# The first SwiGLU chunk of an encoder layer takes its weight sums from the last stage's two buffers

## The chip, the cores and the metric

The kernel runs on one core of one Trainium2 chip. The metric is device time in microseconds (us), the median of the runs shown.

## What is computed

One post-norm encoder layer over 256 positions of width 2048, in float32: a combined projection feeding a convolution group, a pooling group and a Fourier group, an output projection, LayerNorm, then the part that matters here:

```
hid = silu(x @ w_gate) * (x @ w_up)            # 2048 -> 5632
ffn = hid @ w_down                             # 5632 -> 2048
ple = sigmoid(x @ w_ple_gate) * (p @ w_ple)
x   = layer_norm(ALPHA * x + ffn + ple, ln2_g, ln2_b)
```

## The kernel before

Weights stream from HBM as tiles of 128 x 2048 float32 (1 MB). Every tile is taken apart into a high and a low part: a cast on ACT (`whi`, L125) and a subtraction on DVE (`wlo`, L126), each on half a tile (128 x 1024). For every 128 rows of weights `mm3` (L163 to L165) then issues three 128x128x512 matmuls on PE: high by high, low by high, high by low.

All streamed weight tiles go through the pool `wraw`, which has four buffers with the name `raw`. SP issues the loads in one queue; a load waits until the buffer's last reader is done, and the loads behind it wait with it.

The stage ahead of SwiGLU is the gate projection of `ple` (`w_pg`, four chunks of 512 columns). Each of its chunks ends with a sigmoid on ACT (L543), a product with `ple` (L544) and an update of the residual (L545) on DVE. Its tiles (`sg2`, `ple0`, `ple1` and others) are in the pool `ple`. When this pool and the pool `conv` are closed, the last stage's pool `ffn` is laid over the same memory.

SwiGLU (`hidden`) goes over 11 chunks of 512 hidden columns. Each chunk makes the two products x W_gate and x W_up as a Strassen-like scheme, for which sums of weight tiles are needed: `b11` is gate tile 0, `b12` is up tile 0, and `tsum = b11 + b12` is made by DVE (L592). After that a DMA from POOL adds up tile 1 onto `b12` in place (L593). Later `tsum` gets `b22` (up tile 1) added (L604) and then, by another POOL DMA, gate tile 1 (L606). So `b12` and `tsum` are held for most of a chunk. In chunks 1 to 10 they are in `ffn`, in two buffers named `sraw`. In chunk 0 they are two of the four `raw` buffers, and the other tiles of chunk 0 pass through the two that are left.

PE's order in a chunk is: `b11` (12 matmuls onto X), `tsum` (12, onto Z), up tile 2 (24), `tsum` again (12), `b22` (12), up tile 3 (24), `b12` (12), then gate tile 2 (24), gate tile 1 (12), `tsum` (12) and gate tile 3 (24): 180 in all. The order of instructions on each engine is fixed when the program is built.

Of the kernel before, what the change touches and what calls it, by code (L numbers as in the profile page):

```python
# [9 lines left out]
F32 = mybir.dt.float32  # L10
# [6 lines left out]
P = 128  # L17
# [7 lines left out]
NC = 512  # L25
# [63 lines left out]
def encoder_layer(ctx: ExitStack, tc, t):  # L89
    nc = tc.nc  # L90
    cpool = ctx.enter_context(tc.tile_pool(name="const", bufs=1))
    wraw = ctx.enter_context(tc.tile_pool(name="wraw", bufs=4))
# [27 lines left out]
    def load(out, in_):  # L120
        last_load[0] = nc.sync.dma_start(out, in_)
# [427 lines left out]
    with tc.tile_pool(name="ffn", bufs=1) as ffn:  # L549
        st = [small.tile([P, 8, 6], F32, name=f"st2{j}", tag=f"st2{j}") for j in range(NT)]  # L550

        def x1q(j, q):

            a = slice((q % 2) * 4, (q % 2) * 4 + 4)
            return x1hi[q // 2][:, a, j * P : (j + 1) * P], x1lo[q // 2][:, a, j * P : (j + 1) * P]

        def form(i):
            return fhi[:, i], flo[:, i]

        def fetch(dram, u, pool, tag, bufs):  # L560
            raw = pool.tile([P, 4 * NC], F32, name=tag, tag=tag, bufs=bufs)
            load(raw, dram[u])
            return raw

        def multiply(raw, uses):

            for h in range(0, 4, 2):
                hi = wsp.tile([P, 2, NC], F32R, name="whi", tag="whi")
                lo = wsp.tile([P, 2, NC], F32R, name="wlo", tag="wlo")
                split(raw[:, h * NC : (h + 2) * NC].rearrange("p (k n) -> p k n", n=NC), hi, lo)  # L570
                for k in range(2):
                    for out, (ahi, alo), start, stop in uses:
                        mm3(
                            out, ahi[:, h + k, :], alo[:, h + k, :], hi[:, k, :], lo[:, k, :],
                            start and h + k == 0, stop and h + k == 3, skip_group_check=True,
                        )

        def kept(src):
            out = ffn.tile([P, NC], F32, name="sgl", tag="sgl", bufs=6)
            nc.scalar.copy(out, src)  # L580
            return out

        def hidden(c, pool, tag, bufs):


            acc = lambda: pacc.tile([P, NC], F32, name="acc", tag="acc")
            gate, up = t["w_gate"][c], t["w_up"][c]
            X, Z = acc(), acc()
            b11 = fetch(gate, 0, wraw, "raw", None)
            b12 = fetch(up, 0, pool, tag, bufs)  # L590
            tsum = pool.tile([P, 4 * NC], F32, name=tag, tag=tag, bufs=bufs)
            nc.vector.tensor_tensor(tsum, b11, b12, op=ALU.add)  # L592
            nc.gpsimd.dma_start(b12, up[1], accum_op=ALU.add)  # L593
            multiply(b11, [(X, x1q(0, 0), True, True)])
            W = acc()
            nc.scalar.copy(W, X)
            multiply(tsum, [(Z, form(0), True, True)])
            while deferred:
                deferred.pop(0)()
            s5 = kept(Z)  # L600
            V = acc()
            multiply(fetch(up, 2, wraw, "raw", None), [(V, x1q(1, 2), True, False), (Z, x1q(0, 2), False, False)])
            b22 = fetch(up, 1, wraw, "raw", None)
            nc.vector.tensor_tensor(tsum, tsum, b22, op=ALU.add)  # L604
            multiply(tsum, [(X, form(1), False, True)])
            nc.gpsimd.dma_start(tsum, gate[1], accum_op=ALU.add)  # L606
            s16 = kept(X)
            multiply(b22, [(Z, form(3), False, False)])
            multiply(fetch(up, 3, wraw, "raw", None), [(V, x1q(1, 3), False, True), (Z, x1q(0, 3), False, True)])
            multiply(b12, [(X, form(2), False, True)])  # L610

            nc.vector.tensor_tensor(s16, Z, s16, op=ALU.subtract)
            nc.vector.tensor_tensor(s5, s5, X, op=ALU.subtract)
            nc.vector.tensor_tensor(s5, V, s5, op=ALU.add)
            multiply(fetch(gate, 2, wraw, "raw", None), [(W, x1q(0, 2), False, False), (X, x1q(1, 2), False, False)])
            multiply(fetch(gate, 1, wraw, "raw", None), [(W, x1q(0, 1), False, False)])
            multiply(tsum, [(X, x1q(1, 1), False, False)])
            multiply(fetch(gate, 3, wraw, "raw", None), [(W, x1q(0, 3), False, True), (X, x1q(1, 3), False, True)])
            hh = ffn.tile([P, 4, S], F32R, name="hhi", tag="hhi", bufs=4)
            hl = ffn.tile([P, 4, S], F32R, name="hlo", tag="hlo", bufs=4)  # L620

            def end():
                sg = gates(c)
                for s, p in zip(sg, (W, X)):
                    nc.scalar.activation(s, p, AF.Silu)
                gated(c, sg, (s16, s5), hh, hl)

            deferred.append(end)
            return hh, hl

        def gates(c):

            tag, bufs = ("keep", 2) if c in PAIRS else ("sgl", 6)
            return [ffn.tile([P, NC], F32, name=tag, tag=tag, bufs=bufs) for _ in range(NT)]
# [7 lines left out]
        def gated(c, g, v, hh, hl):  # L642

            for j in range(NT):
                nc.vector.tensor_tensor(g[j], v[j], g[j], op=ALU.mult)
                if c not in PAIRS or j == 0:
                    js = slice(j * P, (j + 1) * P)
                    turn(g[j], hh[:, :, js], hl[:, :, js])
            if c in PAIRS:
                first[:] = [g, hh, hl]  # L650
            if c - 1 in PAIRS:
                (a11, a21), ph, pl = first
                a12, a22 = g
                fh, fl = (ffn.tile([P, 3, 4, P], F32R, name=n, tag=n) for n in ("dfh", "dfl"))
                tail = slice(P, S)
                for a, b, op, out, hi, lo in (
                    (a21, a22, ALU.subtract, a22, ph[:, :, tail], pl[:, :, tail]),
                    (a11, a21, ALU.subtract, a21, fh[:, 1], fl[:, 1]),
                    (a22, a11, ALU.subtract, a11, fh[:, 0], fl[:, 0]),
                    (a12, a11, ALU.add, a12, fh[:, 2], fl[:, 2]),  # L660
                ):
                    nc.vector.tensor_tensor(out, a, b, op=op)
                    turn(out, hi, lo)
                sums_of[c - 1] = [(ph[:, :, tail], pl[:, :, tail])] + [(fh[:, i], fl[:, i]) for i in range(3)]
# [50 lines left out]

        first, sums_of = [], {}
        for part in ((0, 4), (4, 8), (8, 11)):
            hid = [hidden(c, *((ffn, "sraw", 2) if c else (wraw, "raw", None))) for c in range(*part)]
            if part[1] == 11:
                g2, b2 = (ffn.tile([P, D], F32, name="sraw", tag="sraw", bufs=2) for _ in range(2))  # L720
                for b, row in ((g2, t["ln2_g"]), (b2, t["ln2_b"])):
                    nc.sync.dma_start(b, row.partition_broadcast(P))
            nk = 4 * len(hid)
            last = part[1] == 11
            if not last:
                for c in (0, 2):
                    down_pair(c, part[0], hid)
                continue
            for c in range(4):
                ps = project(  # L730
                    t["w_down"][c][part[0] : part[1]], nk,
                    lambda k: (hid[k // 4][0][:, k % 4, :], hid[k // 4][1][:, k % 4, :]),
                    behind=16 if c == 3 else 0, spare=12 if c == 3 else 0, halves=c == 3,
                )
                for j in range(NT):
                    for h in range(2):
                        cc = slice(c * NC + h * S, c * NC + (h + 1) * S)
                        src = ps[j][:, h * S : (h + 1) * S] if j == 0 or c < 3 else ps[1 + h][:, :S]
                        nc.vector.tensor_tensor(res[j][:, cc], src, res[j][:, cc], op=ALU.add)
                        nc.vector.bn_stats(st[j][:, 2 * c + h, :], res[j][:, cc])  # L740
# [108 lines left out]
```

## Time and profile before

| what | value |
|---|---|
| median of 3 runs | 1079.39 us (1079.01 to 1079.45) |
| the profiled execution: its time | 1079.06 us |
| the profiled execution: its span | 1077.3 us |
| PE busy | 1055.2 us (98%) |
| DVE busy | 878.7 us (82%) |
| ACT busy | 646.5 us (60%) |
| mean rate of the DMAs | 229 GB/s |

The span is the time between the first and the last instruction of the profiled execution; 1.8 us of its time lie outside the span. PE is a chain of matmuls with short gaps, so what counts is where PE waits, and for whom.

### The profile page before, as it was taken

The numbers are of one execution on the slowest core, as the hardware profiler recorded it, in microseconds if no ns is written. First come the engines' busy times: TensorE is split into PE (matmuls) and PEld (weight loads), VectorE is DVE, ScalarE is ACT, GpSimd is POOL, SyncE is SP. The second block draws the span as 40 slices with busy tenths as digits, with TensorE's granted clock in tenths as the row PEclk, the third lists the DMA queues.
The fourth block names the chain that finished last, engine by engine and source line by source line (L and its number), as shares of the span: only waits on it lengthen the run. The fifth ranks groups of instructions, "written<-read, shape, count | busy, mean of one in ns | idle before, by whom it ended". The sixth has DMA issues, their size and how long they took to land.

```text
span 1077.3 us, 12568 instructions
## 1 busy us (share of the span) xinstructions
PE 1055.2 (98%) x4692; PEld 857.5 (80%) x4692; DVE 878.7 (82%) x1021; ACT 646.5 (60%) x810; POOL 30.9 (3%) x56
## 2 busy tenths in 40 slices
PE   7999999999999999999999999999999999999995
PEld 6888878887788878888887888888887878888884
DVE  5899999969956768888879778798788787887576
ACT  6888876636644656666655556566655565665440
POOL 0000000000000000000000000000000000000000
PEclk9999999999999999999999999999999999999998
DMA  9777543644554788678787786777787877868432
GB/s 355 283 280 219 196 156 137 241 159 177 196 195 159 227 274 302 210 239 270 233 273 224 246 294 199 252 262 231 245 248 259 273 212 249 291 199 321 176 115 78
DMA packets 36801, 246.62 MB, mean 229 GB/s; under 512 B 4188, under 2 KB 4740, under 8 KB 7940
## 3 DMA queue, kind: packets, MB, share of 16 engines
q1 hardware_dynamic: 32004, 212.25, 51.5%
q0 software_dynamic: 4736, 33.57, 16.8%
q8 instruction: 37, 0.61, 0.2%
q14 instruction: 24, 0.20, 0.1%
HBM read 243.70 MB, written 2.10 MB: 228 GB/s over the span
## 4 chain that ended last, share of the span: by engine, by line
PE 90%; DVE 6%; DMA 1%; ACT 1%; issue 1%; SPq 0%; DVEq 0%; ACTq 0%
PE acc L164 29%; PE acc L163 29%; PE acc L165 29%; DVE wlo L126 2%; PE tp L639 1%; ACT whi L125 1%; DMA raw<-in_w_gate 1%; DMA raw<-in_w_in 1%; PE tp L448 1%; DVE res L744 0%; DVE res L749 0%; DVE sraw L695 0%; DVE sraw L604 0%; DVE res L506 0%; PE tp L403 0%
## 5 line engine op out<-in xcount | busy, mean ns | idle before, releaser
L126 DVE TENSOR_TENSOR wlo<-raw,whi 128x1024 fp32r<-128x1024 f32 (+1 forms) x354 | 423.5, 1214 | 116.4 <-ACT whi L125 112.7
L125 ACT CAST whi<-raw 128x1024 fp32r<-128x1024 f32 (+1 forms) x354 | 369.7, 1048 | 234.8 <-PE acc L165 212.2
L163 PE MATMUL acc<-whi,ahi 128*128 128x512 f32 x1108 | 435.3, 395 | 6.8 <-ACT whi L125 5.5
L164 PE MATMUL acc<-wlo,ahi 128*128 128x512 f32 x1108 | 435.0, 393 | 1.0 <-DVE wlo L126 0.9
L165 PE MATMUL acc<-whi,alo 128*128 128x512 f32 x1108 | 431.6, 391 | 0.1
L163 PEld LDWEIGHTS acc<-whi,ahi 128*128 128x128 f32 x1108 | 208.6, 188 | 54.9 <-ACT whi L125 6.4
L164 PEld LDWEIGHTS acc<-wlo,ahi 128*128 128x128 f32 x1108 | 208.5, 188 | 48.4 <-DVE wlo L126 6.6
L165 PEld LDWEIGHTS acc<-whi,alo 128*128 128x128 f32 x1108 | 208.4, 188 | 43.6 <-DVE alo L126 0.4
L125 ACT CAST whi<-sraw 128x1024 fp32r<-128x1024 f32 x112 | 116.5, 1053 | 91.6 <-PE acc L165 55.3
L126 DVE TENSOR_TENSOR wlo<-sraw,whi 128x1024 fp32r<-128x1024 f32 x112 | 135.0, 1221 | 43.5 <-ACT whi L125 43.1
L164 PE MATMUL acc<-wlo,hhi 128*128 128x512 f32 x264 | 104.5, 396 | 0.0
L165 PE MATMUL acc<-whi,hlo 128*128 128x512 f32 x264 | 103.6, 395 | 0.0
L163 PE MATMUL acc<-whi,hhi 128*128 128x512 f32 x264 | 103.5, 397 | 0.0
L281 ACT ACTIVATE pr<-uT,par 128x256 f32<-128x256 f32 x128 | 56.8, 501 | 5.6 <-DVE part L283 5.4
L163 PEld LDWEIGHTS acc<-whi,hhi 128*128 128x128 f32 x264 | 49.6, 188 | 12.7 <-DVE res L676 1.2
L164 PEld LDWEIGHTS acc<-wlo,hhi 128*128 128x128 f32 x264 | 49.7, 188 | 12.1 <-DVE wlo L126 1.0
L165 PEld LDWEIGHTS acc<-whi,hlo 128*128 128x128 f32 x264 | 49.7, 188 | 11.6
L287 DVE SCALAR_TENSOR_TENSOR mixc<-uT,par,mixc 128x256 f32<-128x256 f32 x104 | 46.4, 474 | 0.0
L283 DVE TENSOR_TENSOR part<-part,pr 128x512 f32<-128x512 f32 x64 | 43.5, 680 | 0.3 <-ACT pr L281 0.2
L592 DVE TENSOR_TENSOR sraw<-raw,sraw 128x2048 f32<-128x2048 f32 x10 | 22.9, 2292 | 0.3
L604 DVE TENSOR_TENSOR sraw<-sraw,raw 128x2048 f32<-128x2048 f32 x10 | 22.9, 2286 | 0.1
L580 ACT COPY sgl<-acc 128x512 f32<-128x512 f32 x22 | 12.9, 588 | 14.5 <-PE acc L165 13.2
(148 smaller groups left out, 630.2 us busy)
## 6 DMA issues: line engine op xcount, KB each, us to landing
raw<-in_w_gate SPq DMA_DIRECT2D x44, 1024.0 KB, 7.3
raw<-in_w_down SPq DMA_DIRECT2D x40, 1024.0 KB, 5.0
raw<-in_w_up SPq DMA_DIRECT2D x34, 1024.0 KB, 4.9
raw<-in_w_in SPq DMA_DIRECT2D x22, 1024.0 KB, 5.0
raw<-in_w_out SPq DMA_DIRECT2D x16, 1024.0 KB, 4.8
raw<-in_w_pg SPq DMA_DIRECT2D x16, 1024.0 KB, 4.9
sraw<-in_w_up SPq DMA_DIRECT2D x10, 1024.0 KB, 6.9
sraw<-in_w_up POOLq DMA_DIRECT2D x10, 1024.0 KB, 9.3
```

The lines of the kernel that those rows point to most:

```text
L125: nc.scalar.copy(hi, src)
L126: return nc.vector.tensor_tensor(lo, src, hi.bitcast(F32), op=ALU.subtract)
L163: nc.tensor.matmul(out, ahi, whi, start=start, stop=False, **more)
L164: nc.tensor.matmul(out, ahi, wlo, start=False, stop=False, **more)
L165: nc.tensor.matmul(out, alo, whi, start=False, stop=stop, **more)
L281: nc.scalar.mul(pr[:, n, :], uT[ch][:, k : k + S], w)
L283: nc.vector.tensor_tensor(part, part, pr, op=ALU.add)
L287: nc.vector.scalar_tensor_tensor(y[ch], in0=uT[ch][:, k : k + S], scalar=w, in1=y[ch], op0=ALU.mult, op1=ALU.add)
L448: nc.tensor.matmul(out, ones, x, start=i == 0, stop=i == NCH - 1)
L580: nc.scalar.copy(out, src)
L592: nc.vector.tensor_tensor(tsum, b11, b12, op=ALU.add)
L604: nc.vector.tensor_tensor(tsum, tsum, b22, op=ALU.add)
```

## The change

Chunk 0 takes `b12` and `tsum` from `ffn` like the other chunks. The parameters that told the chunks apart are gone.

```
-        def hidden(c, pool, tag, bufs):
+        def hidden(c):
...
             b11 = fetch(gate, 0, wraw, "raw", None)
-            b12 = fetch(up, 0, pool, tag, bufs)
-            tsum = pool.tile([P, 4 * NC], F32, name=tag, tag=tag, bufs=bufs)
+            b12 = fetch(up, 0, ffn, "sraw", 2)
+            tsum = ffn.tile([P, 4 * NC], F32, name="sraw", tag="sraw", bufs=2)
             nc.vector.tensor_tensor(tsum, b11, b12, op=ALU.add)
             nc.gpsimd.dma_start(b12, up[1], accum_op=ALU.add)
...
-            hid = [hidden(c, *((ffn, "sraw", 2) if c else (wraw, "raw", None))) for c in range(*part)]
+            hid = [hidden(c) for c in range(*part)]
```

The buffers of a pool are laid out in the order in which they are first asked for. `sraw` was first asked for in chunk 1, behind `sgl`, `hhi` and `hlo`; now it is the first of `ffn`.

SP's queue, from the load of `b11` (raw_3085) on. Before, with `b12` as raw_3087 and the first `sraw` load that of chunk 1 (sraw_3390); what a load waits for is in brackets (DVE and Activation are counts of those engines' instructions, DMAHW and DMASW those of earlier DMAs):

```order
L121 DMA raw_3085<-in_w_gate 128x2048 [waits DMAHW5_49,DVE_49]
L121 DMA raw_3087<-in_w_up 128x2048 [waits DMAHW6_49,DVE_49]
L121 DMA raw_3137<-in_w_up 128x2048 [waits DMAHW0_49,DVE_49]
L121 DMA raw_3171<-in_w_up 128x2048 [waits DMAHW1_49,DVE_49]
L121 DMA sraw_3390<-in_w_up 128x2048 [waits DMASW1_49,DMASW2_49,DMASW0_49,DMASW3_49,DVE_49,Activation_49]
L121 DMA raw_3217<-in_w_up 128x2048 [waits DMAHW3_49,DVE_49]
```

The change, with `b12` as sraw_3087:

```order
L121 DMA raw_3085<-in_w_gate 128x2048 [waits DMAHW5_49,DVE_49]
L121 DMA raw_3137<-in_w_up 128x2048 [waits DMAHW6_49,DVE_49]
L121 DMA raw_3171<-in_w_up 128x2048 [waits DMAHW7_49,DVE_49]
L121 DMA raw_3217<-in_w_up 128x2048 [waits DMAHW0_49,DVE_49]
L121 DMA sraw_3087<-in_w_up 128x2048 [waits DMASW1_49,DMASW2_49,DMASW0_49,DMASW3_49,DVE_49,Activation_49]
L121 DMA raw_3274<-in_w_gate 128x2048 [waits DMAHW1_49,DVE_49]
```

The load of `b12` went from second place to fifth, behind three tiles that are multiplied after it, and it has taken over the wait that chunk 1's load had as the first one into `ffn`. In the built program the counts in that wait are those of the last L545 and the last L543 of the stage before, in both kernels alike.

DVE's order around the end of the `w_pg` stage. Before:

```order
L592 TENSOR_TENSOR raw_3089<-raw_3085,raw_3087 128x2048
L126 TENSOR_TENSOR wlo_3037<-raw_3034,whi_3036 128x1024
L126 TENSOR_TENSOR wlo_3053<-raw_3034,whi_3052 128x1024
L126 TENSOR_TENSOR wlo_3093<-raw_3085,whi_3092 128x1024
L126 TENSOR_TENSOR wlo_3103<-raw_3085,whi_3102 128x1024
L126 TENSOR_TENSOR wlo_3115<-raw_3089,whi_3114 128x1024
L544 TENSOR_TENSOR sg2_3068<-sg2_3068,ple0_2280 128x512
L544 TENSOR_TENSOR sg2_3072<-sg2_3072,ple1_2281 128x512
L545 SCALAR_TENSOR_TENSOR res0_485<-res0_485,sg2_3068 128x512
L545 SCALAR_TENSOR_TENSOR res1_486<-res1_486,sg2_3072 128x512
L126 TENSOR_TENSOR wlo_3125<-raw_3089,whi_3124 128x1024
```

The change:

```order
L126 TENSOR_TENSOR wlo_3093<-raw_3085,whi_3092 128x1024
L126 TENSOR_TENSOR wlo_3103<-raw_3085,whi_3102 128x1024
L544 TENSOR_TENSOR sg2_3068<-sg2_3068,ple0_2280 128x512
L544 TENSOR_TENSOR sg2_3072<-sg2_3072,ple1_2281 128x512
L545 SCALAR_TENSOR_TENSOR res0_485<-res0_485,sg2_3068 128x512
L545 SCALAR_TENSOR_TENSOR res1_486<-res1_486,sg2_3072 128x512
L592 TENSOR_TENSOR sraw_3089<-raw_3085,sraw_3087 128x2048
L126 TENSOR_TENSOR wlo_3115<-sraw_3089,whi_3114 128x1024
L126 TENSOR_TENSOR wlo_3125<-sraw_3089,whi_3124 128x1024
L126 TENSOR_TENSOR wlo_3140<-raw_3137,whi_3139 128x1024
```

The sum `tsum` (L592, here raw_3089 and sraw_3089) and the subtraction for its first half (wlo_3115) went from ahead of the last L544 and L545 to behind them.

PE's order stays as it was but for one matmul of gate tile 3, which trades places with the two ahead of it. Here is the change where the first product with `tsum` begins (whi_3114 is the cast of its first half, acc_3083 is X, acc_3084 is Z; for this place the waits are shown):

```order
L164 MATMUL acc_3083<-wlo_3103,ahi_2370 128x512
L165 MATMUL acc_3083<-whi_3102,alo_2372 128x512
L163 MATMUL acc_3084<-whi_3114,ahi_2770 128x512 [waits Activation_49]
L164 MATMUL acc_3084<-wlo_3115,ahi_2770 128x512 [waits DVE_49]
L165 MATMUL acc_3084<-whi_3114,alo_2771 128x512
```

Nothing moved here: the 12 matmuls of `tsum` stand right behind the 12 of `b11` and ahead of the 24 of up tile 2, in both kernels.

## Rows read from the trace of the kernel before

**Rows 1.** The page, parts 1 and 4: busy time; the chain by engine.
```profile
PE 1055.2 (98%) x4692; PEld 857.5 (80%) x4692; DVE 878.7 (82%) x1021; ACT 646.5 (60%) x810; POOL 30.9 (3%) x56
...
PE 90%; DVE 6%; DMA 1%; ACT 1%; issue 1%; SPq 0%; DVEq 0%; ACTq 0%
```

**Rows 2.** Busy time by stage: window, length, engines, PE clock, DMA share, GB/s.
```profile
358.00:402.00 44.00, 42.18 (x184) 33.89 (x183) 34.54 (x32) 26.42 (x29) 1.72 (x2) 1.00 0.78 250
402.00:1077.00 675.00, 662.24 (x2958) 537.25 (x2956) 545.05 (x540) 384.29 (x413) 23.32 (x27) 0.99 0.73 236
```

**Rows 3.** PE in order of time in chunk 0: start, duration, instruction, idle before.
```profile
358.54 0.39 PE L163 MATMUL acc<-whi,ahi 128*128 128x512 f32 x1
...
376.09 0.39 PE L165 MATMUL acc<-whi,alo 128*128 128x512 f32 x1
...
378.13 0.39 PE L165 MATMUL acc<-whi,alo 128*128 128x512 f32 x1
...
384.03 0.50 PE L164 MATMUL acc<-wlo,ahi 128*128 128x512 f32 x1 [0.53 <-DVE wlo L126]
...
387.50 0.50 PE L163 MATMUL acc<-whi,ahi 128*128 128x512 f32 x1 [1.23 <-DVE sgl L613]
...
404.85 0.60 PE L639 MATMUL tp<-ident,keep 128*128 128x128 f32 x4
```

**Rows 4.** The chain of waits in chunk 0: start, duration, what.
```profile
364.68 2.21 DVE raw L604
366.91 1.06 ACT whi L125
...
372.65 8.91 DMA raw<-in_w_gate
```

**Rows 5.** SP's queue in order of time: start, duration, load.
```profile
350.20 0.33 SPq L121 DMA_DIRECT2D raw<-in_w_up  x1
...
361.33 0.33 SPq L121 DMA_DIRECT2D sraw<-in_w_up  x1
```

**Rows 6.** What SP's queue waited for, 330 to 400: total, times, longest.
```profile
SPq L121 <- DVE res L545: 5.2, 1, 5.2
```

**Rows 7.** DVE in order of time around the end of the stage before.
```profile
345.61 2.29 DVE L592 TENSOR_TENSOR raw<-raw 128x2048 f32<-128x2048 f32 x1 [0.88 <-DMA raw<-in_w_up]
...
354.39 1.23 DVE L126 TENSOR_TENSOR wlo<-raw,whi 128x1024 fp32r<-128x1024 f32 x1 [1.50 <-ACT whi L125]
...
359.99 1.28 DVE L545 SCALAR_TENSOR_TENSOR res<-res,sg 128x512 f32<-128x512 f32 x2
```

**Rows 8.** DMA issues from 340 to 346: size, us from issue to landing.
```profile
raw<-in_w_up SPq DMA_DIRECT2D x1, 1024.0 KB, 4.8
```

**Rows 9.** The page, part 6: DMA issues, whole span, median to landing.
```profile
sraw<-in_w_up SPq DMA_DIRECT2D x10, 1024.0 KB, 6.9
sraw<-in_w_up POOLq DMA_DIRECT2D x10, 1024.0 KB, 9.3
```

**Rows 10.** PE in order of time at the start of the program.
```profile
5.15 0.79 PE L163 MATMUL acc<-whi,ahi 128*128 128x512 f32 x1 [5.15 <-ACT whi L125]
...
6.90 0.63 PE L163 MATMUL acc<-whi,ahi 128*128 128x512 f32 x1
7.33 0.63 PE L164 MATMUL acc<-wlo,ahi 128*128 128x512 f32 x1
...
9.42 0.39 PE L163 MATMUL acc<-whi,ahi 128*128 128x512 f32 x1
```

**Rows 11.** Busy time in windows at the start and the end (PE's last matmul is in the second).
```profile
4.00:8.00 4.00, 2.85 (x6) 2.04 (x7) 2.15 (x4) 2.54 (x5) 0.00 (x0) 1.00 0.93 294
...
1064.00:1066.00 2.00, 0.74 (x7) 0.53 (x5) 1.97 (x4) 0.00 (x0) 0.00 (x0) 1.00 0.75 281
1066.00:1070.00 4.00, 0.00 (x0) 0.00 (x0) 3.93 (x11) 0.00 (x0) 0.00 (x0) 0.69 0.34 122
1070.00:1077.00 7.00, 0.00 (x0) 0.00 (x0) 3.65 (x9) 0.00 (x0) 0.00 (x0) 0.50 0.41 150
```

## The prediction

> **What bounds the kernel now.** Read the busy times and the chain first: PE is busy for 98% of the span and makes 90% of the chain [rows 1]. So a change costs what it adds to PE's waits, gains what it takes from them, and anything else is hidden. The table by stage comes next: from 358 to 402 us, chunk 0 of SwiGLU, PE is busy for 42.18 of 44 us; the 675 us after it lose 12.8 us [rows 2], 12 of them behind PE's last matmul [rows 11]. The edit touches chunk 0 alone. Then PE in order of time gives what chunk 0 loses. Nine matmuls take 2.04 us when nothing disturbs PE (376.09 to 378.13), a pitch of 0.2267 us. Chunk 0's first matmul starts at 358.54 and the first transpose behind chunk 0 and the 12 of chunk 1's `b11` at 404.85, 192 matmuls later [rows 3]. At the pitch that is 43.5 us; it took 46.3. **Chunk 0 loses 2.8 us**, and the idle marks show where: around 384 and 387 us. The chain says why: at 372.65 a load of a gate tile is issued and takes 8.9 us to be there [rows 4]. It was issued late because only two `raw` buffers were turning over.
>
> **What the change can give.** With four `raw` buffers, gate tile 2 gets the buffer of `b11` as soon as the sum L592 is made, some 20 us before PE wants it. I count the whole 2.8 us as gained. It can't be more, since the rest of the chunk is at PE's pitch.
>
> **What it adds: a wait at the start of the chunk.** Before, the sum L592 was made at 345.61 us [rows 7], 13 us ahead of chunk 0. Now its input `b12` is the first load into `ffn`. That position existed before: it was chunk 1's load, issued at 361.33 [rows 5], after SP had waited 5.2 us for L545 [rows 6], which ends at 359.99 + 1.28 = 361.27 [rows 7]. There it cost nothing, since chunk 1 is 40 us later. Chunk 0's `tsum` is wanted 12 matmuls after the chunk's start. Nothing ahead of L545 is moved that PE waits for, so I keep these times and work forward:
>
> - PE runs out of `b11` at 358.54 + 12 x 0.2267 = 361.26.
> - The load of `b12` is issued at 361.33. Its three neighbours in the queue are long out (the last of them waits for a subtraction that was done when SP went on at 350.20 [rows 5]), so it runs alone. The load of the same tile took 4.8 us alone [rows 8]: there at 366.1. The bound from above is the median of loads into `sraw` among others, 6.9 us [rows 9]. I take 4.8, since nothing else is in flight then.
> - L592 began 0.14 us after its load was there (340.67 + 4.8 against 345.61) and takes 2.29 us [rows 7]: 366.3 to 368.6.
> - ACT's cast of the first half starts at once and takes 1.06 us, as it did behind L604 [rows 4]: done at 369.7. PE's first matmul on `tsum` starts there, 8.4 us after it ran dry.
> - The second matmul needs the low part: DVE's subtraction takes 1.23 us [rows 7], so 370.95. The second half's cast and subtraction follow on their engines and are done by 372.2, in time.
> - At the pitch, matmul 12 of `tsum` would end the stretch so that up tile 2 starts at 373.45. Without any wait it starts at 358.54 + 24 x 0.2267 = 363.98. **The wait costs 9.5 us** at full clock.
>
> PE's order is fixed, with `tsum` ahead of up tile 2, so the three tiles that are already there can't fill this hole.
>
> **The clock.** After PE's last matmul near the end of the program the granted clock falls: 1.00 to 1066, a mean of 0.69 to 1070, then 0.50 [rows 11]; with levels 1 and 0.5 the fall is 1.5 us into that window, about 3 us after the last matmul. A hole of 8.4 us is longer. What the return costs is seen at the program's start: the matmuls of the first 4.3 us (5.15 to 9.42) follow each other at 0.43 us instead of 0.23 (6.90 to 7.33) [rows 10], which is 512 columns at 1.2 GHz. If the lower level again holds for 4.3 us from 369.7, that is to 374.0, matmuls 2 to 9 of `tsum` stand 0.43 apart from 370.95 on (the ninth at 373.94), the last three 0.23 apart, and up tile 2 starts at 374.86: **1.4 us more**, since part of the slow time lies under the wait for the low part. Only one thing in the trace speaks against it: the clock column shows 1.00 for 4 to 8 us [rows 11], where the matmuls stand at the lower pitch. The Trainium skill (TensorE: Matmul & The Clock Gate, section on the HAM clock gate) holds that the throttled state is the default and that activity releases it. By that rule the early 1.00 is not a granted clock at all, only the absence of a recorded change, and the 1.4 us stand; by the column taken literally the start was slow for another reason and the sum would be 1.4 us less. I go by the pitch.
>
> **What comes after.** Everything behind is shifted by 10.9 us and needs less than it has. DVE's queue from 369.7 on is 4 subtractions and L604, done near 377; the product that needs it starts after up tile 2, at 380.3. The POOL DMA onto `b12` starts after L592 at 368.6 and takes 9.3 us [rows 9]; it is wanted at 391. Gate tile 2 is issued at 368.6 too and wanted at 394. Chunk 1's load into `sraw` moves from 361.33 to behind chunk 0's last use of `b12`, at about 392; it lands before 400 and is wanted at 408. That is the steady state of chunks 2 on, where PE stays at its pitch. Nothing later wins back time: PE is the bound there. The other edits (a buffer's place in memory, the wait of the first `sgl` write, which no longer meets a fresh pool) cost nothing, as they lie beside matmuls.
>
> **The sum.** 9.5 + 1.4 - 2.8 = +8.1 us. The profiled execution took 1079.06 us, so 1087.2; the median of the runs shown is 0.33 above it, so **1087.5 us**, 0.75% slower. A measurement of this kernel can tell about 0.2%, 2.2 us, from no change.
>
> **The rivals.**
>
> - *The clock holds, or most of its loss lies under the waits.* For it: the clock column at the start. Against it: the pitch there, and the fall at the end. +6.7 us: 1086.1. Chance 0.13.
> - *The load is not alone or is slow*, at 6.9 us [rows 9] or with a longer time at the lower clock. 2.1 us more: 1089.6. Against it: the queue is empty at 361. Chance 0.14.
> - *Not slower: the load of `b12` does not wait for L545.* The memory it now gets, the first of `ffn`, held tiles of `conv` and not the sigmoid's. If the load went out right behind its neighbour, near 350, it would be there by 357, and all that is left is DVE's order: L592 stands behind L545, 361.27 to 363.56, the cast to 364.65, the subtraction to 365.9, up tile 2 at 368.4. That costs 4.4 us against 2.8 won: +1.6, 1081.0, no change that can be told. It decides at one point: the load must be there by 361.3. Against it stands the order of the change, where the load carries the same DVE and ACT waits that chunk 1's had, and [rows 6], where that wait is seen to bind. Chance 0.04.
> - *Faster*: L592 would have to be early as well, and DVE's order excludes it. Chance 0.01.
>
> The forecast keeps 0.68. Slower by over 0.2%: 0.95; within 0.2%: 0.04; faster: 0.01. The range of 8 in 10 holds the forecast with its own bounds (a landing of 4.4 to 6 us, 0 to 3 us of clock) and the first two rivals: 1085.5 to 1090.
>
> **What would show it.** In the profile of the change: SP's load into `sraw` at about 361.3, released by L545; L592 at 366.3 with an idle DVE ahead of it; PE's idle mark of about 8 us ended by ACT's cast, in the chunk's 13th matmul; matmuls 0.43 us apart behind it; a granted clock below 1 somewhere between 364 and 376; and no idle marks where 384 and 387 were. I am wrong if L592 starts before 363 (then the third rival), if the hole is above 10 us (the second), or if the stretch from 404.85 on is longer than before by more than its shift, which would be a wait that I have missed.

## The result, and the profile after

The change is slower: 1088.36 us (median of 4 runs, 1087.93 to 1089.25) against 1079.42 us for the kernel before on the same chip, a ratio of 1.008 (95% interval 1.0068 to 1.0092). That is 8.9 us; 8.1 were forecast.

The page of the change, parts 1 and 4, answers to [rows 1]: PE works 2 us longer, over a span that is 9 us longer.

```profile
PE 1057.2 (97%) x4692; PEld 858.8 (79%) x4692; DVE 879.7 (81%) x1021; ACT 646.9 (60%) x810; POOL 30.9 (3%) x56
...
PE 91%; DVE 5%; DMA 1%; ACT 1%; issue 1%; SPq 0%; DVEq 0%; ACTq 0%
```

PE in order of time (start, duration, instruction, idle before), which answers to [rows 3]: `b11`'s first matmul, its last, then those of `tsum`, the first of up tile 2 at 375.44, and the transpose that [rows 3] end with.

```profile
358.77 0.39 PE L163 MATMUL acc<-whi,ahi 128*128 128x512 f32 x1
...
361.27 0.39 PE L165 MATMUL acc<-whi,alo 128*128 128x512 f32 x1
369.94 0.80 PE L163 MATMUL acc<-whi,ahi 128*128 128x512 f32 x1 [8.28 <-ACT whi L125]
371.20 0.80 PE L164 MATMUL acc<-wlo,ahi 128*128 128x512 f32 x1 [0.46 <-DVE wlo L126]
371.79 0.63 PE L165 MATMUL acc<-whi,alo 128*128 128x512 f32 x1
372.22 0.63 PE L163 MATMUL acc<-whi,ahi 128*128 128x512 f32 x1
...
374.75 0.40 PE L163 MATMUL acc<-whi,ahi 128*128 128x512 f32 x1
...
375.44 0.39 PE L163 MATMUL acc<-whi,ahi 128*128 128x512 f32 x1
...
414.04 0.60 PE L639 MATMUL tp<-ident,keep 128*128 128x128 f32 x4
```

From the first matmul to the transpose it is 55.27 us, against 46.31 before: 8.96 us more, which is the whole result. I use this stretch below, because the chunk's own start moves by up to 0.8 us from profile to profile.

The chain of waits across the hole shows who made it. Each line is a start, a duration and what ran: the load goes out when L545 is done, then the sum, then ACT's cast.

```profile
360.82 0.70 DVE res L545
361.51 0.02 SPq L121
361.54 0.03 issue
361.57 4.78 DMA sraw<-in_w_up
366.35 0.03 issue
366.38 0.05 DVEq L592
366.43 0.04 issue
366.47 2.30 DVE sraw L592
368.78 0.03 ACTq L125
368.80 0.04 issue
368.84 1.05 ACT whi L125
```

What SP's queue waited for between 330 and 400 us, which answers to [rows 6]: the wait for L545 is twice as long, since three loads that stood behind `b12` are out earlier and nothing is left to do ahead of it.

```profile
SPq L121 <- DVE res L545: 10.6, 1, 10.6
```

The busy times by window (the granted PE clock is the third number from the end) show the clock falling inside the hole and coming back about 5 us after PE does:

```profile
361.50:364.00 2.50, 0.15 (x1) 0.00 (x0) 0.00 (x1) 0.57 (x1) 0.00 (x0) 1.00 0.52 131
364.00:366.00 2.00, 0.00 (x0) 0.00 (x0) 0.00 (x0) 0.00 (x0) 0.00 (x0) 0.62 0.85 360
366.00:368.00 2.00, 0.00 (x0) 0.00 (x0) 1.53 (x1) 0.00 (x0) 0.00 (x0) 0.50 0.00 0
...
372.00:374.00 2.00, 2.00 (x6) 1.54 (x6) 2.00 (x3) 0.73 (x1) 0.00 (x0) 0.50 1.07 291
374.00:376.00 2.00, 2.00 (x9) 1.64 (x8) 2.00 (x2) 0.36 (x1) 0.00 (x0) 0.82 0.99 193
376.00:378.00 2.00, 2.00 (x10) 1.51 (x9) 0.83 (x2) 1.39 (x3) 0.00 (x0) 1.00 0.98 205
```

In the rest of the chunk PE has no idle mark: the ones at 384 and 387 us of [rows 3] are gone. From up tile 2 to the transpose it takes 38.60 us; before it took 40.87 (363.98 to 404.85).

### The profile page after: what moved, and what is told of

Read it like the earlier page. It is cut to its first block, busy times and chain, and to the rows that moved or that the text cites. A ratio compares the mean times of both kernels' runs of the same rounds, so it can differ in the third digit from the quotient of the medians.

```text
span 1086.3 us, 12568 instructions
## 1 busy us (share of the span) xinstructions
PE 1057.2 (97%) x4692; PEld 858.8 (79%) x4692; DVE 879.7 (81%) x1021; ACT 646.9 (60%) x810; POOL 30.9 (3%) x56
## 4 chain that ended last, share of the span: by engine, by line
PE 91%; DVE 5%; DMA 1%; ACT 1%; issue 1%; SPq 0%; DVEq 0%; ACTq 0%
PE acc L164 29%; PE acc L163 29%; PE acc L165 29%; PE tp L639 1%; DVE wlo L126 1%; ACT whi L125 1%; DMA raw<-in_w_in 1%; PE tp L448 1%; DVE res L744 0%; DVE res L749 0%; DMA sraw<-in_w_up 0%; DVE sraw L695 0%; DVE sraw L604 0%; DVE res L506 0%; PE tp L403 0%
## 5 line engine op out<-in xcount | busy, mean ns | idle before, releaser
L126 DVE TENSOR_TENSOR wlo<-raw,whi 128x1024 fp32r<-128x1024 f32 (+1 forms) x346 | 414.7, 1214 | 113.7 <-ACT whi L125 110.1
L125 ACT CAST whi<-raw 128x1024 fp32r<-128x1024 f32 (+1 forms) x346 | 362.2, 1048 | 226.1 <-PE acc L165 211.6
L125 ACT CAST whi<-sraw 128x1024 fp32r<-128x1024 f32 x120 | 124.8, 1053 | 102.7 <-PE acc L165 52.5
L126 DVE TENSOR_TENSOR wlo<-sraw,whi 128x1024 fp32r<-128x1024 f32 x120 | 144.6, 1222 | 46.8 <-ACT whi L125 46.5
L592 DVE TENSOR_TENSOR sraw<-raw,sraw 128x2048 f32<-128x2048 f32 x11 | 25.2, 2293 | 5.3 <-DMA sraw<-in_w_up 5.0
L604 DVE TENSOR_TENSOR sraw<-sraw,raw 128x2048 f32<-128x2048 f32 x11 | 25.1, 2286 | 0.1
L593 POOL DMA_DIRECT2D sraw<-in_w_up x11 | 9.5, 863 | 527.9 <-DVE sraw L592 309.0
```

Source lines behind the costliest of these rows:

```text
L125: nc.scalar.copy(hi, src)
L126: return nc.vector.tensor_tensor(lo, src, hi.bitcast(F32), op=ALU.subtract)
```

## The experiments

The theory: the load of `b12` waits for the last instruction of the pool that had this memory, and so makes a hole in PE that the clock makes dearer; what two more `raw` buffers give is smaller. The rivals are the place in memory, the order of the sum on DVE alone, and a clock that costs nothing. The table has the stretch from `b11`'s first matmul to the transpose in each run's trace (one execution each), and the ratio to the kernel before in the same comparison.

| kernel | stretch, us | ratio, 95% interval |
|---|---|---|
| before | 46.31 | |
| the change | 55.27 | 1.008 (1.0068 to 1.0092) |
| e1_place | 46.63 | 0.9999 (0.999 to 1.0007) |
| e2_use | 56.07 | 1.0083 (1.0069 to 1.0096) |
| e3_warm | 53.61 | 1.0066 (1.0054 to 1.0079) |
| e4_tsum | 50.05 | 1.0045 (1.0031 to 1.0059) |
| e5_b12 | 55.88 | 1.0087 (1.0073 to 1.0101) |
| e6_early | 44.50 | 0.9973 (0.9963 to 0.9984) |
| e7_inplace | 44.92 | 0.9985 (0.9976 to 0.9993) |

### Place or use

The change does two things at once: chunk 0 uses the buffers, and the buffers come to lie first in `ffn`. Each was tried alone. Added to the kernel before, ahead of the loop over the chunks (`e1_place`):

```
+        for _ in range(2):
+            ffn.tile([P, 4 * NC], F32, name="sraw", tag="sraw", bufs=2)
```

> The kernel before, with the last stage's memory laid out as in the change (its two buffers first) and chunk 0 still in its four raw buffers. If the loss is the wait of chunk 0's load for the stage before (my theory), the place costs nothing: 1079.4 us, within 1 us, no hole at 361 us. If the place in memory is what costs (rival: other chunks meet other waits), most of the 9 us appear here: 1085 to 1089.

Measured: 1079.57 us against 1079.98, no difference. PE keeps the old idle marks and gets no new one:

```profile
384.43 0.50 PE L164 MATMUL acc<-wlo,ahi 128*128 128x512 f32 x1 [0.76 <-DVE wlo L126]
387.89 0.50 PE L163 MATMUL acc<-whi,ahi 128*128 128x512 f32 x1 [1.23 <-DVE sgl L613]
```

The other half, added to the change (`e2_use`):

```
+        ffn.tile([P, NC], F32, name="sgl", tag="sgl", bufs=6)
+        for n in ("hhi", "hlo"):
+            ffn.tile([P, 4, S], F32R, name=n, tag=n, bufs=4)
```

> The change, with the last stage's memory laid out as before (the two buffers behind the others, where the sigmoid's products of the stage before were). My theory: as the change, 1088.4 us, a hole of 8 to 9 us from 361 us that ends with the load issued after L545. Rival of the place: 1079.4 us. A rival by addresses (only memory that was really in use late is waited for): the same 1088.4 here, but then the change itself could not have waited, since its two buffers lie where nothing of the sigmoid was.

Measured: 1088.78 us, as the change. SP's queue and then PE in order of time:

```profile
361.83 0.33 SPq L121 DMA_DIRECT2D sraw<-in_w_up  x1
```

```profile
370.28 0.79 PE L163 MATMUL acc<-whi,ahi 128*128 128x512 f32 x1 [8.36 <-ACT whi L125]
```

The stretch is 0.8 us longer than in the change, mostly because the clock stays low until 376.4 us, some 6 us from PE's return; that need not be an effect of the place, as the low clock differs as much between executions of one and the same code (see the last section). The place costs nothing and the use costs everything. Together the two runs show one thing more. By the addresses in the built programs, the buffer of `b12` lies in this run over tiles of the pool `ple` (`praw`, `pehi`, `pelo` and the start of `ple0`), and in the change over `conv`'s `par`, `ones` and the start of `mixc`, which is last read at 289 us. Neither lies over bytes that the last L543 to L545 use, and yet the load waits for L545 in both. The wait belongs to the pools that were closed, not to the bytes.

### The clock

The change, with PE kept busy through most of the hole (`e3_warm`); the extra products go to a bank that nobody reads:

```
             nc.scalar.copy(W, X)
+            if c == 0:
+                idle = ptp.tile([P, NC], F32, name="tp", tag="tp")
+                for _ in range(34):
+                    nc.tensor.matmul(idle, x1hi[0][:, 0, :P], x1hi[0][:, 0:2, :], start=True, stop=True)
             multiply(tsum, [(Z, form(0), True, True)])
```

> The change, with 34 extra matmuls onto an unused bank between the products of b11 and of tsum, so that PE is busy for 7.7 us of the hole; their result is not used. If the lower clock behind the hole costs what was read from the pitch, the granted clock stays at 1.00, the matmuls of tsum stand 0.23 apart, and up tile 2 starts about 1.5 us sooner: 1086.9 us. If the clock costs nothing (rival), 1088.4; if the extra matmuls delay the chunk, more.

Measured: 1087.07 us, 1.3 less than the change, though from another chip; on the same chip as this run, `e2_use` took 1088.78. The intervals of the ratios overlap, but the slowest execution here (1087.19) is faster than the fastest of either (1087.93 and 1088.31). Within the traces it is plainer. PE in order of time, from two answers:

```profile
361.98 7.64 PE L600 MATMUL tp<-ahi 128*128 128x512 f32 x33
...
370.41 0.51 PE L163 MATMUL acc<-whi,ahi 128*128 128x512 f32 x1 [0.78 <-ACT whi L125]
371.67 0.51 PE L164 MATMUL acc<-wlo,ahi 128*128 128x512 f32 x1 [0.76 <-DVE wlo L126]
372.01 0.40 PE L165 MATMUL acc<-whi,alo 128*128 128x512 f32 x1
```

The 13th matmul from 370.41 on, up tile 2's first, starts at 374.30. The chunk began at 359.26 here, so this is 15.04 us into it, against 16.67 in the change: the clock's price is 1.6 us. What is left, 15.04 less the 5.44 of 24 matmuls at the pitch, is 9.6 us: the wait at full clock. The granted clock is 1.00 in every window of this run from 361 to 378 us.

### Half of the change

Only `tsum` in `ffn` (`e4_tsum`), which takes the load out of the wait and leaves the sum behind L545:

```
             b12 = fetch(up, 0, pool, tag, bufs)
-            tsum = pool.tile([P, 4 * NC], F32, name=tag, tag=tag, bufs=bufs)
+            tsum = ffn.tile([P, 4 * NC], F32, name="sraw", tag="sraw", bufs=2)
```

> Half of the change: chunk 0's tsum in the last stage's memory, b12 in a raw buffer as before. This is the prediction's third rival made real: the load of b12 is early, and only DVE's sum stands behind L545. Theory: L592 at 361.5 us instead of 366.5, PE's hole 3.4 us instead of 8.3, up tile 2 some 4.4 us late if the clock holds; the idle at 384 and 387 us mostly gone, as three raw buffers turn over: 2.1 us above before, 1081.5; 1.4 us more, 1083, if the clock falls in so short a hole. Rival (the load's wait is not what makes the hole): as the change, 1088.

Measured: 1083.92 us against 1079.48, half of the loss, and a little more than expected. PE's hole is 3.35 us, as worked out (PE in order of time, then the clock by windows):

```profile
365.40 0.50 PE L163 MATMUL acc<-whi,ahi 128*128 128x512 f32 x1 [3.35 <-ACT whi L125]
366.67 0.79 PE L164 MATMUL acc<-wlo,ahi 128*128 128x512 f32 x1 [0.76 <-DVE wlo L126]
367.26 0.63 PE L165 MATMUL acc<-whi,alo 128*128 128x512 f32 x1
...
369.76 0.39 PE L165 MATMUL acc<-whi,alo 128*128 128x512 f32 x1
```

```profile
364.00:366.00 2.00, 0.50 (x1) 0.19 (x1) 0.85 (x2) 1.69 (x2) 0.86 (x1) 1.00 0.99 414
366.00:368.00 2.00, 1.33 (x3) 1.15 (x4) 2.00 (x3) 2.00 (x3) 0.00 (x0) 0.57 1.05 369
368.00:370.00 2.00, 2.00 (x7) 1.53 (x7) 2.00 (x3) 0.19 (x1) 0.00 (x0) 0.58 1.00 246
```

The clock fell here too, and only when PE had begun again: behind the hole there is one matmul and a second wait, of 0.76 us, and the fall lies within 366 to 368. Up tile 2 starts 11.49 us into the chunk (359.18 to 370.67), 6.0 us late instead of the 4.4 that were worked out for full clock. So the third rival of the prediction, made real, would not have been "no change": with the clock it is 0.45% slower. Of the 11.2 us by which up tile 2 is late in the change (375.44 less 358.77, less 5.44), the sum's place behind L545 with its share of the clock makes 6.0, and the load's late issue and landing the other 5.2; the split is as rough as the time at the low clock, which differs from execution to execution.

Only `b12` in `ffn` (`e5_b12`):

```
-            b12 = fetch(up, 0, pool, tag, bufs)
+            b12 = fetch(up, 0, ffn, "sraw", 2)
             tsum = pool.tile([P, 4 * NC], F32, name=tag, tag=tag, bufs=bufs)
```

> The other half: b12 in the last stage's memory, tsum in a raw buffer. The load of b12 then stands second in SP's queue, ahead of the three up tiles, which wait with it until 361.5 us. Theory: the hole begins at 361 us as in the change, and is longer, because four loads start at once and because up tile 2 is late as well: 1089 to 1093 us. Rival (only the sum's place in DVE's order counts): as the run with tsum alone, 1081 to 1083.

Measured: 1088.88 us. The rival is out: with the load behind L545 the loss is that of the whole change, wherever the sum lies. But my expectation was too dark as well. Five loads go out within 8 us, the first two of them into `ffn` (`b12` and chunk 1's), and yet the first is not slowed by the others. SP in order of time, and the DMAs of 361 to 372 us (size, median to landing):

```profile
362.12 0.80 SPq L121 DMA_DIRECT2D sraw<-in_w_up  x2
362.98 6.67 SPq L121 DMA_DIRECT2D raw<-in_w_up  x3
```

```profile
raw<-in_w_up SPq DMA_DIRECT2D x3, 1024.0 KB, 10.8
sraw<-in_w_up SPq DMA_DIRECT2D x2, 1024.0 KB, 5.8
```

PE's hole is 8.26 us, no longer than in the change. The up tiles take 10.8 us, and up tile 2 still comes in time, because `tsum` itself is so late.

### A version that keeps the gain without the wait

If the theory holds, the gain of the buffers can be had from memory that never lay under a closed pool. The tile `mixc`, which holds the convolution's result and later parts of the transposed `x`, is as large as one weight tile. It is last read at 289 us, about a quarter into the `w_pg` stage, three of its chunks ahead of SwiGLU and not two as expected. In `e6_early` it and every chunk's `b12` share one buffer of a pool that is open throughout; `ffn` gives up one of its two buffers for it, and chunk 0's `tsum` is in a `raw` buffer:

```
+    sums2 = ctx.enter_context(tc.tile_pool(name="sums2", bufs=1))
...
-        mixc = conv.tile([P, 8, S], F32, name="mixc")
+        mixc = sums2.tile([P, 8, S], F32, name="mixc", tag="b12")
...
-            b12 = fetch(up, 0, ffn, "sraw", 2)
-            tsum = ffn.tile([P, 4 * NC], F32, name="sraw", tag="sraw", bufs=2)
+            b12 = fetch(up, 0, sums2, "b12", 1)
+            if c:
+                tsum = ffn.tile([P, 4 * NC], F32, name="sraw", tag="sraw", bufs=1)
+            else:
+                tsum = wraw.tile([P, 4 * NC], F32, name="raw", tag="raw")
...
-            b12 = fetch(w1, p0, ffn, "sraw", 2)
-            tsum = ffn.tile([P, 4 * NC], F32, name="sraw", tag="sraw", bufs=2)
+            b12 = fetch(w1, p0, sums2, "b12", 1)
+            tsum = ffn.tile([P, 4 * NC], F32, name="sraw", tag="sraw", bufs=1)
...
-                g2, b2 = (ffn.tile([P, D], F32, name="sraw", tag="sraw", bufs=2) for _ in range(2))
+                g2 = sums2.tile([P, D], F32, name="b12", tag="b12")
+                b2 = ffn.tile([P, D], F32, name="sraw", tag="sraw", bufs=1)
```

> b12 in memory that is never under a closed pool: one buffer of a pool of its own, whose first tile is the convolution's result (last read two chunks of w_pg before SwiGLU), so its load may go out early; chunk 0's tsum in a raw buffer, of which three are left to turn over instead of two. My theory: no hole at 361 us, and the idle at 384 and 387 us goes too, as gate tile 2 is issued some 7 us sooner: 2.8 us less than before, 1076.6 us, between 1076 and 1077.5. Rival: the 2.8 us are not the buffers but the traffic of the POOL DMAs; then 1079.4.

Measured: 1077.2 us against 1079.98, a ratio of 0.9973 (0.9963 to 0.9984): faster than both kernels. The load of `b12` goes out at 289.40 us and nothing waits for it; gate tile 2 is issued at 364.92 instead of 372.65 (SP in order of time; lines stand one lower here):

```profile
289.40 0.33 SPq L122 DMA_DIRECT2D b<-in_w_up  x1
...
364.92 10.88 SPq L122 DMA_DIRECT2D raw<-in_w_gate  x3
```

Of PE's idle marks in the chunk one is left, from a wait for DVE:

```profile
385.86 0.50 PE L164 MATMUL acc<-whi,ahi 128*128 128x512 f32 x1 [0.56 <-DVE sgl L617]
```

The stretch is 44.50 us, 1.8 less than before and 1.0 above 192 matmuls at the pitch. The expected 1076.6 lies within what the interval leaves; in the trace a third of the 2.8 us stayed.

The last run (`e7_inplace`) also writes chunk 0's `tsum` over `b11`, so that it needs no buffer of its own and the up tiles go out sooner (from 341.09 us instead of 345.48):

```
-                tsum = wraw.tile([P, 4 * NC], F32, name="raw", tag="raw")
+                tsum = b11
+                multiply(b11, [(X, x1q(0, 0), True, True)])
             nc.vector.tensor_tensor(tsum, b11, b12, op=ALU.add)
             nc.gpsimd.dma_start(b12, up[1], accum_op=ALU.add)
-            multiply(b11, [(X, x1q(0, 0), True, True)])
+            if c:
+                multiply(b11, [(X, x1q(0, 0), True, True)])
```

> The early b12 of the run e6_early, and chunk 0's tsum written over b11 in place, which frees one more raw buffer for the tiles behind. Theory: no hole at 361 us; the rest of the idle at 385 us goes (0.6 us there), but the sum can only be made after b11's second subtraction, so the low part of its second half comes behind L545 and costs about 1.3 us near 363: between 1076.5 and 1078, not to be told from e6_early. Rival: every further free buffer is worth as much as the first, 1075.

Measured: 1077.88 us against 1079.48, a ratio of 0.9985 (0.9976 to 0.9993). The mark at 385 us is gone and one at 364 has come in its place, as DVE reaches the second half's subtraction only behind L545:

```profile
364.38 0.50 PE L165 MATMUL acc<-wlo,ahi 128*128 128x512 f32 x1 [0.72 <-DVE wlo L127]
```

The intervals of the two versions overlap, so which is the better one stays open; the rival of 1075 us is out.

## Why the prediction was right

- **The wait, forecast 9.5 us at full clock.** Right: 9.6 us by `e3_warm`. Its pieces in the change are the forecast ones, 0.2 us later throughout: load at 361.57 (361.33 forecast), 4.78 us to landing (4.8), sum at 366.47 (366.3), first matmul at 369.94 (369.7), idle 8.28 us (8.4). That the load would run alone held.
- **The clock, forecast 1.4 us.** Right in kind, a little short: 1.6 us. The low level held from 369.94 to 374.75, 4.8 us, where 4.3 were taken from the start of the program. That one reading came so near is partly luck: at the start the low pitch lasts 3.4 us in the trace of `e3_warm` and 6.0 in that of `e2_use`, and by the prediction's working these would have given 1.0 and 2.2 us. The range had room for either. The choice between the pitch and the clock column was right: in the change the column itself shows 0.50 where the matmuls stand 0.43 us apart, so the same pitch at the start speaks for the low level there, whatever the 1.00 beside it means; no run tests the column there. The Trainium skill (TensorE: Matmul & The Clock Gate, section on the HAM clock gate) holds that the throttled state is the default, and the pitch of 0.43 us at the start agrees with this.
- **The gain, forecast 2.8 us.** This is the term that was mis-sized: 40.87 us became 38.60 from up tile 2 on, 2.3 us. "It can't be more" was right; counting all of it was not. 168 matmuls at the pitch are 38.1 us, and the 0.5 us that remain are slips too short for an idle mark. Nor are all of the 2.3 us shown to come from the buffers alone, as the chunk also runs 11 us late: with three buffers and no lateness (`e6_early`) the same part takes 39.06 us (364.19 to 403.25), with three and 6 us of lateness (`e4_tsum`) 38.56.
- **What comes after.** Nothing later was late, and nothing won the time back, as forecast.
- **The sum.** 9.6 + 1.6 - 2.3 = 8.9 against 8.96 in the trace and 8.94 between the medians. The forecast of 8.1 was low by the three small errors, all on the same side. That the trace's terms close is no proof of its own, since they are cut from one stretch; what `e3_warm` adds is the split between wait and clock.
- **The rivals.** The clock that holds would have been 6.7 us, the slow load 10.2; the trace excludes both. The third one's condition, a load that is there by 361.3 us, was made true in `e4_tsum`. It falls in another way than I gave: even then the kernel is 4.4 us slower, since the clock also fell there, behind a hole of 3.35 us, one matmul and a wait of 0.76 us.

## What to carry to other kernels

When a tile moves to a pool that is laid over a closed one, ask what the closed pool did last, not what lay at that address: the first load waits for all of it, and what is wanted next to that seam should be in memory that stays open across it. A buffer that an earlier stage has finished with, and that is as large as the tile, can be shared by giving both one pool; in `e6_early` no cost of that is seen. And cost a hole in PE by its length and by the clock behind it.

## What was not expected of the hardware

After a hole the low clock lasts a different time from case to case, counted from PE's return: 4.8 us in the change, some 6 us in `e2_use`, and in `e5_b12` 6.5 us, from 370.48 until the matmul at 377.02 (PE in order of time):

```profile
376.60 0.62 PE L163 MATMUL acc<-whi,ahi 128*128 128x512 f32 x1
377.02 0.43 PE L164 MATMUL acc<-wlo,ahi 128*128 128x512 f32 x1
377.29 0.39 PE L165 MATMUL acc<-whi,alo 128*128 128x512 f32 x1
```

It does so without any difference in the code as well. The program's first stage is the same in the kernel before, `e3_warm` and `e2_use`, and there the matmuls stood 0.43 us apart for 4.3, 3.4 and 6.0 us. In the last two the pitch changes at these lines, the first pair from `e3_warm` (first matmul at 5.64), the second from `e2_use` (at 5.30):

```profile
8.66 0.56 PE L163 MATMUL acc<-whi,ahi 128*128 128x512 f32 x1
9.06 0.39 PE L164 MATMUL acc<-wlo,ahi 128*128 128x512 f32 x1
```

```profile
11.32 0.47 PE L164 MATMUL acc<-wlo,ahi 128*128 128x512 f32 x1
11.63 0.40 PE L165 MATMUL acc<-whi,alo 128*128 128x512 f32 x1
```

So one trace gives the price of a fallen clock only roughly: the estimate above runs from 1.0 to 2.2 us.

In `e4_tsum` the fall came after PE had already begun again, so a short hole can cost more than its length. And of the five 1 MB loads issued in one row in `e5_b12`, the first landed in about the time that it takes alone (the sum starts at 367.00, 4.9 us after the load's issue). The median of the first two is 5.8 us, that of the three behind them 10.8 us.
